# Two column blocks of an output projection by Strassen's seven products

## The chip, the core and the metric

One core of a Trainium2 chip. The metric is the device time of one execution in microseconds; lower is better. The runs of the kernel before took 1024.64, 1024.73 and 1025.47 us, median 1024.73.

## The reference

One layer of a hybrid encoder on 512 frames (tokens) of width 2048. One input projection feeds two groups of heads, RWKV-7 time mixing and an HGRN2 gated recurrence; their gated outputs are put side by side and go through one output projection, a scaled residual and a LayerNorm:

```python
proj = jnp.einsum('btd,dc->btc', h, w_in[l])
rw = _token_shift(proj[..., :RWKV_COLS], shift_mu[l])
hg = proj[..., RWKV_COLS:]
o_rwkv, v_first = _rwkv7_branch(rw, ...)
o_hgrn = _hgrn2_branch(hg, ...)
y = jnp.einsum('btc,cd->btd', jnp.concatenate([o_rwkv, o_hgrn], axis=-1), w_out[l])
h = _layer_norm(ALPHA * h + y, ln_w[l], ln_b[l])
```

The change lies in the last `einsum`: (512 x 2048) times (2048 x 2048), in float32.

## The kernel before, in words

**One wide matmul.** Float32 products are made of TensorE matmuls on `float32r` halves: every operand is split into a high part (a copy by ACT into `float32r`) and a low part (the rest, a subtraction by DVE), in `split` (L367 for ACT, L377 for DVE). `three` (L499) then issues high x high, high x low and low x high into the same PSUM bank. So a product of a 128x128 stationary tile and a 128x512 moving tile is three wide matmuls.

**Stages.** The head (L1317) multiplies the first pieces of x and of the weights while they arrive. Then come the input projections, one after another, each 48 wide matmuls by `proj` (L499); between them the planner places the narrow matmuls of the two recurrences (L353). Last comes the output projection, in four column blocks of 512 (d = 0 to 3). For d = 0, 1 and 2 all four token tiles are accumulated in four PSUM banks, and the loop goes over 16 depth steps: a weight tile of 128x512 serves 4 token tiles x 3 = 12 matmuls. The last block goes token tile by token tile, with its 16 weight tiles kept split in SBUF; they were loaded and split alternately with those of d = 2 (`_last_quarters`). Its last token tile is cut in two column halves for the last four depth steps, so that the serial chain behind the last matmul (statistics, LayerNorm, store) is short.

**What sets the order.** The Python program is a planner: class `Plan` keeps a clock for each engine, and generators in queues (`splits`, `evacs`, `sums`, ...) yield operations with an assumed cost. `three` advances PE's clock and calls `pump`, which issues whatever is ready by the clocks. The order on each engine is therefore fixed when the kernel is built. A narrow matmul is issued when its operands are due 0.35 us ahead (`LEAD`). At run time engines meet by semaphores alone, each in its own fixed order.

**Weights.** `load(j)` sends 512 KB (two weight tiles) from `w_all` into one of two `wr` buffers, on SP's queue, once the buffer two loads back has been split. The split tiles go into a ring of three `wh`/`wl` buffers. SP's queue also carries the head's pieces, all other loads, the spills (`spill`: 12 of the 16 gated outputs rest in DRAM until the output projection), the passes through DRAM that transpose (`far`), the residual (`x_r`) and the stores of the result.

**Evacuation.** `row_out` adds the scaled residual to the PSUM bank on DVE (L390) and writes a `y` tile; statistics follow (L1581), and `finish` normalizes a token tile once its last column block is in (DVE L377, ACT L1510). `finish_last` does so for the last tile.

GpSimd does little before: clears (L419), powers for the square roots (L416), and one addition of 128x512 in the tail (L409).

Of the kernel before, what the change touches and what calls it, by code (L numbers as in the profile page):

```python
# [7 lines left out]
F32 = mybir.dt.float32  # L8
# [7 lines left out]
P = 128  # L16
# [246 lines left out]
def mixer_kernel(ctx, tc, head, x_r, w_all, par, up, ln_wb, consts, hmask, out):  # L263
# [212 lines left out]
    def ready(i, home=None):

        if i < 2 * nload and i not in parts:
# [444 lines left out]
    def rwkv_scan(SS, sc):  # L923
# [16 lines left out]
        for c in range(NCH):  # L940
# [321 lines left out]

    us = [unit() for _ in range(FIRST)]
# [58 lines left out]
    for k in range(KT):  # L1322
# [60 lines left out]
    def split_gated(n):  # L1383
        while len(whole) < min(n, KT):
# [68 lines left out]
    lnw = []  # L1453
# [60 lines left out]
    def finish_last(t, pbs, weigh):  # L1514
# [4 lines left out]
        dg = st("ksq", [P, T])[:, :P]  # L1519
        yield from spread(t, mv, rs, 5)  # L1520
# [48 lines left out]

    def row_out(t, d, ps):  # L1570
        y = ys[t][d] = yt[4 * t + d]
        xr = xrs[t]
        k = y_keys(t, d * T, d * T + T)

        def run():
            yield keyed(stt(y, xr, ALPHA, ps, ALU.mult, ALU.add), [xr.tensor.name, ps.tensor.name], k + [y.tensor.name])
            drop(ps, xr)
            plan.add(sums, rest())

        def rest():  # L1580
            yield keyed(Op([("dve", 0.07 + T * 0.00105, lambda: dve.bn_stats(stats[:, t, d], y))], [], []),  # L1581
                        k, [f"stat{t}"])
            if d == 3:
                yield from finish(t)
            else:
                yield from premultiply(t, d)

        plan.add(evacs, run())

    xrs = {}  # L1590

    def residual(t, d):
# [11 lines left out]

    def ahead(j, d):

        if d == 0:
            split_gated(j + 2)
            if j == 8:
                plan.until(room(big=1))  # L1610
                lnw.append(take("big", [P, 2, D]))
                send(lnw[0], ln_wb[None].to_broadcast([P, 2, D]))
                plan.fetched(lnw[0], 8 * D)
# [4 lines left out]
    for d in range(2):  # L1618
        rows(4 * unit(4), T, gh, gl, lambda t, ps, d=d: fin(t, ps, d), korder, lambda j, d=d: ahead(j, d),
             banks if d else banks[:1])  # L1620

    q0 = 4 * unit(8)
    seq = _last_quarters()
    homes = {}

    def home(n):
        if n < 9:
            return lambda: tuple(take("t", (P, QT), F32R) for _ in range(2))  # L1630
        if n == 9:
# [5 lines left out]
        if n == 10:  # L1637
            return lambda: tuple(take("ksq", (P, QT), F32R) for _ in range(2))
        if n < 13:
            def both():  # L1640
                if not homes:
# [167 lines left out]
```

## Time and profile before

| | |
|---|---|
| median of three runs | 1024.73 us |
| the profiled execution | 1025.05 us |
| its span, first to last instruction | 1023.3 us |
| instructions | 18559 |
| granted TensorE clock, mean | 0.999 |
| HBM read, written | 111.08 MB, 18.48 MB |

The profile is one execution. Its engines are PE (TensorE matmuls), PEld (TensorE weight loads, which run beside PE), DVE (VectorE), ACT (ScalarE), POOL (GpSimd) and SP (SyncE, which issues DMAs). A group row has line, engine, operation, out<-in by tile names, shapes and count, then the busy time in us and the mean of one in ns, then the idle time before and who ended it. A timeline row has start and length in us. Matmuls overlap, so the length of one (393 ns) is not the distance to the next. "PEclk" is the granted clock as a share of full speed.

### The profile page before, as it was taken

How to read it: one execution, taken by the hardware profiler on the slowest of the kernel's cores; microseconds unless marked ns; L12 is line 12 of the kernel's file. 1: busy time of each engine (PE TensorE's matmuls, PEld its weight loads, DVE VectorE, ACT ScalarE, POOL GpSimd, SP SyncE). 2: the span in 40 equal slices, each digit the busy share in tenths (PEclk: the TensorE clock that was granted, in tenths of full speed). 3: DMA queues.
4: the chain of work that ended last, by engine and by line, in shares of the span. 5: the costliest groups of instructions: out<-in, count | busy, mean ns of one | idle time of the engine just before them, and what ended most of it. 6: DMA issues, size and time to landing. Idle time of an engine off the chain costs nothing.

```text
span 1023.3 us, 18559 instructions
## 1 busy us (share of the span) xinstructions
PE 1015.0 (99%) x7124; PEld 839.5 (82%) x7124; DVE 805.0 (79%) x1753; ACT 474.6 (46%) x879; POOL 42.8 (4%) x78
## 2 busy tenths in 40 slices
PE   9999999999999999999999999999999999999997
PEld 8888888888888878888888888888888878888885
DVE  7477999779779979888999867867999988526556
ACT  6456345546373454555534353636345554223321
POOL 0000001001000010010001000100001001000001
PEclk9999999999999999999999999999999999999999
DMA  9134452342535422335463333363343247445613
GB/s 340 54 103 129 124 143 83 96 124 88 177 106 155 124 84 63 100 113 166 121 182 105 100 98 116 106 187 103 119 128 94 78 142 237 144 119 169 202 55 134
DMA packets 58553, 130.77 MB, mean 128 GB/s; under 512 B 9824, under 2 KB 25440, under 8 KB 58336
## 3 DMA queue, kind: packets, MB, share of 16 engines
q1 hardware_dynamic: 58032, 128.67, 42.1%
q8 instruction: 56, 0.92, 0.4%
q10 hardware_dynamic: 432, 0.92, 0.3%
q14 instruction: 33, 0.27, 0.1%
HBM read 111.08 MB, written 18.48 MB: 127 GB/s over the span
## 4 chain that ended last, share of the span: by engine, by line
PE 95%; DVE 3%; issue 1%; DMA 0%; ACT 0%; DVEq 0%; ACTq 0%; SPq 0%
PE main L499 73%; PE mix L353 9%; PE mix L499 8%; PE main L1317 3%; PE main L353 2%; DVE t L377 1%; DVE wl L377 1%; PE mix L1268 0%; DMA t<-spill 0%; DVE bd L390 0%; DVE big L403 0%; DVE inv L403 0%; DVE zz L377 0%; PE mix L358 0%; DVE nr L398 0%
## 5 line engine op out<-in xcount | busy, mean ns | idle before, releaser
L499 PE MATMUL main<-xh,wh 128*128 128x512 f32 x864 | 339.8, 393 | 0.0
L499 PE MATMUL main<-xh,wl 128*128 128x512 f32 x864 | 339.5, 393 | 0.0
L499 PE MATMUL main<-xl,wh 128*128 128x512 f32 x864 | 338.9, 392 | 0.0
L367 ACT ACTIVATE wh<-wr 128x512 fp32r<-128x512 f32 x299 | 186.6, 626 | 190.0 <-PE main L499 128.6
L377 DVE TENSOR_TENSOR wl<-wr,wh 128x512 fp32r<-128x512 f32 x299 | 203.7, 683 | 61.6 <-ACT wh L367 57.4
L499 PEld LDWEIGHTS main<-xh,wl 128*128 128x128 f32 x864 | 162.3, 188 | 33.6
L499 PEld LDWEIGHTS main<-xh,wh 128*128 128x128 f32 x864 | 162.3, 188 | 32.9
L499 PEld LDWEIGHTS main<-xl,wh 128*128 128x128 f32 x864 | 162.4, 188 | 32.9
L499 PE MATMUL main<-wh,xh 128*128 128x512 f32 (+1 forms) x249 | 97.3, 391 | 0.0
L499 PE MATMUL main<-wl,xh 128*128 128x512 f32 (+1 forms) x249 | 97.0, 389 | 0.0
L499 PE MATMUL main<-wh,xl 128*128 128x512 f32 (+1 forms) x249 | 96.5, 388 | 0.0
L499 PEld LDWEIGHTS main<-wh,xh 128*128 128x128 f32 x249 | 46.8, 188 | 9.6
L499 PEld LDWEIGHTS main<-wh,xl 128*128 128x128 f32 x249 | 46.8, 188 | 9.4
L499 PEld LDWEIGHTS main<-wl,xh 128*128 128x128 f32 x249 | 46.8, 188 | 9.2
L368 ACT ACTIVATE t<-main,om 128x512 f32<-128x512 f32 x33 | 22.3, 685 | 46.0 <-PE main L499 35.5
L390 DVE SCALAR_TENSOR_TENSOR bd<-mix,pc,bd 64x64 f32<-64x64 f32 x112 | 31.7, 283 | 12.5 <-PE mix L353 10.4
L377 DVE TENSOR_TENSOR inv<-inv,inv 64x30 f32<-64x30 f32 (+14 forms) x120 | 38.5, 321 | 3.1
L377 DVE TENSOR_TENSOR inv<-inv 64x30 f32<-64x30 f32 (+14 forms) x120 | 38.4, 320 | 2.4
L390 DVE SCALAR_TENSOR_TENSOR t<-main,pr,t 128x511 f32<-128x511 f32 x33 | 24.3, 743 | 17.7 <-ACT t L368 17.3
L377 DVE TENSOR_TENSOR t<-t,tot 128x256 f32<-128x256 f32 x96 | 37.3, 417 | 0.3
L368 ACT ACTIVATE t<-main 128x512 f32<-128x512 f32 x32 | 18.6, 596 | 34.4 <-PE main L499 34.3
L367 ACT ACTIVATE t<-mix 64x128 f32<-64x128 f32 (+3 forms) x57 | 15.0, 267 | 41.1 <-DVE zz L377 25.5
(244 smaller groups left out, 1437.2 us busy)
## 6 DMA issues: line engine op xcount, KB each, us to landing
wr<-w_all SPq DMA_DIRECT2D x156, 512.0 KB, 3.6
q<-head SPq DMA_DIRECT2D x14, 448.0 KB, 5.6
far<-ksq SPq DMA_DIRECT2D x22, 256.0 KB, 3.7
far<-q SPq DMA_DIRECT2D x8, 512.0 KB, 3.7
q<-far SPq DMA_DIRECT2D x32, 128.0 KB, 4.6
g<-x_r SPq DMA_DIRECT2D x16, 256.0 KB, 4.1
t<-far SPq DMA_DIRECT2D x56, 64.0 KB, 3.5
spill<-g SPq DMA_DIRECT2D x12, 256.0 KB, 4.0
```

What stands on the lines that cost most here:

```text
L353: return Op([("pe", cost, lambda: pe.matmul(o, l, r, start=start, stop=stop, **kw))], [l, r], [o], mode=("narrow", l.shape[0], 32 if m <= ...
L367: return "act", cost, lambda: sc_e.activation(o, i, f, scale=scale)
L368: return "act", cost, lambda: sc_e.activation(o, i, f, scale=scale, bias=bias)
L377: return dve_op([a, b], o, lambda: dve.tensor_tensor(o, a, b, f), base=base or 0.16 if o.shape[0] < P and size(o) == C and o.tensor.name i ...
L390: return dve_op([a, b], o, lambda: dve.scalar_tensor_tensor(o, a, s, b, f1, f2), per=0.00113, base=0.085 if o.shape[0] == P and size(o) > ...
L499: pe.matmul(ps, l, r, start=first and i == 0, stop=last and i == 2)
L1317: pe.matmul(pss[a], *ops, start=k == 0 and low == of == 0, stop=k == KT - 1 and low == 1)
```

## The change

**Seven products.** Columns 512 to 1535 (d = 1 and 2) are one 512 x 2048 by 2048 x 1024 product. Depth is cut in two halves: depth tile 2m belongs to the first and 2m + 1 to the second, for m = 0 to 7. Tokens are cut into 0 to 255 and 256 to 511, columns into d = 1 and d = 2. Strassen's method (in Winograd's form) needs seven products of half-size matrices in place of eight. They are the seven passes in `PASSES`. Each goes over 8 depth steps and has 2 PSUM banks, one for each of 2 token tiles, so a weight tile serves 6 matmuls. Three passes use plain weights (`B11`, `B21`, `B22`) and four use sums of weights (0 to 3); three use plain tokens (`A11`, `A12`, `A22`) and four use sums of tokens (`S1` to `S4`). `gather` adds each pass's two banks to the `y` tiles on DVE.

**Weight sums.** `weight_sums`, two loops that start in the head, do this 16 times in all: load 512 KB of `w_all` into an `inv` buffer, form the sums by four subtractions of 128x256 on GpSimd, store 512 KB to `sums_w` in DRAM. All on SP's queue. The passes load the sums from there.

**Token sums.** `union` forms S1 to S4 by four GpSimd operations of 128x256 for each m, as soon as `split_gated` has split the two gated outputs; 12 of those are read a second time from `spill`. `alone` splits the sums into high and low.

**Buffers.** In the passes the ring of weights has a fourth buffer (in `ksq`) and the loads a third (in two `t` tiles, `third`).

**Residual and norm weights.** The residual of these two blocks is scaled by ACT and added to `y` by GpSimd (`join`, 8 additions of 128x512). The LayerNorm's weights are read in four parts after the token sums have been split (`fetch_norm`), no longer in one read in the first block; the early multiplications of the last token tile go into a queue of their own (`weighs`).

**Last block.** Token tiles 0 and 1 are accumulated together, 6 matmuls for a weight tile; tiles 2 and 3 follow as before.

**Elsewhere.** In the recurrence both PSUM banks of a step are taken before its two matmuls are issued.

```diff
+PASSES = (("B11", "A11"), ("B21", "A12"), (3, "S2"), (0, "S1"), ("B22", "S4"), (1, "S3"), (2, "A22"))
...
+            if j < joint or (j - joint) % 3 < 2:
+                t = st("wr", [P, HALF])
+                raws[j] = [t[:, :QT], t[:, QT:]]
+                send(t, source(j))
+                plan.fetched(t, 4 * HALF)
+            else:
+                raws[j] = third
+                for i, t in enumerate(third):
+                    send(t, source(j)[:, i * QT : i * QT + QT])
+                    plan.fetched(t, 4 * QT)
...
-                    load(i // 2 + 2)
+                    load(i // 2 + (2 if i // 2 < joint else 3))
...
+    def weight_sums(first):
+        yield room(inv=1)
+        w = take("inv", [P, 4, QT // 2])
+        for i in range(first, NSUM, 2):
+            m, h = divmod(i, 2)
+            yield lambda: plan.clock["sp"] <= plan.clock["pe"] + 0.2
+            send(w, w_all[nsent + i].rearrange("p (a c) -> p a c", a=4))
+            plan.fetched(w, 4 * HALF)
+            for o, a, b in ((0, 1, 0), (1, 3, 1), (3, 3, 0), (2, 2, 3)):
+                yield pool_tt(w[:, o], w[:, a], w[:, b], ALU.subtract)
+            yield lambda: by_now(w)
+            yield lambda: plan.clock["sp"] <= plan.clock["pe"] + 0.2
+            send(sums_w[:, :, m, h * QT // 2 : (h + 1) * QT // 2].rearrange("a p c -> p a c"), w)
+            there = plan.busy[w.tensor.name] = (plan.clock["sp"] + 4.5, "dma")
+            yield lambda: there[0] <= plan.clock["pe"]
+        drop(w)
...
+        yield pool_tt(d2[:, hi_t], r1[:, hi_t], r2[:, hi_t], ALU.add)
+        yield pool_tt(d1[:, hi_t], r1[:, lo_t], r1[:, hi_t], ALU.subtract)
+        yield pool_tt(d1[:, lo_t], d2[:, hi_t], r1[:, lo_t], ALU.subtract)
+        yield pool_tt(d2[:, lo_t], r2[:, lo_t], d1[:, lo_t], ALU.subtract)
...
+        yield act(xr, xr, AF.Copy, scale=ALPHA)
+        yield keyed(pool_tt(y, ya, xr, ALU.add), ka + [xr.tensor.name], k)
...
+    for p, (_, name) in enumerate(PASSES):
+        pss = []
+        for m in range(NPAIRS):
+            n = parts0 + p * NPAIRS + m
+            hi, lo = part(n, T)
+            for i in range(2):
+                if m == 0:
+                    pss.append(main_ps(banks))
+                prepared(n + 1 + 2 * i)
+                if i == 0:
+                    prepared(n + 2)
+                three(pss[i], *factor(name, m, i), hi[:, 0], lo[:, 0], m == 0, m == NPAIRS - 1)
...
+    for n in range(KT):
+        for t in range(2):
+            if n == 0:
+                pss.append(main_ps(banks))
+            three(pss[t], *shares(t, n, KT - 1))
+    for t in range(2):
+        row_out(t, 3, pss[t])
+    for t in (2, 3):
```

SP's queue behind the head, in the kernel before. `wr` are weights, `up` a small weight of the recurrence, and the brackets name the engines and DMA semaphores an issue waits for:

```order
L332 DMA wr_349<-w_all 128x1024 [waits DMAHW5_49]
L332 DMA wr_414<-w_all 128x1024 [waits DMAHW6_49,DMAHW3_49,DVE_49]
L332 DMA up_445<-up 128x256 [waits DMAHW7_49]
L332 DMA wr_489<-w_all 128x1024 [waits DMAHW5_49,DMAHW0_49,DVE_49]
L332 DMA up_532<-up 128x256 [waits DMAHW1_49,DMAHW7_49,DVE_49,Activation_49]
L332 DMA wr_561<-w_all 128x1024 [waits DMAHW6_49,DMAHW2_49,DVE_49]
```

The same place in the changed kernel; `inv_270` and `inv_271` are the buffers of the two loops:

```order
L332 DMA wr_355<-w_all 128x1024 [waits DMAHW7_49]
L332 DMA sums_w<-inv_270 128x4x256 [waits DMAHW0_49,Pool_49]
L332 DMA sums_w<-inv_271 128x4x256 [waits DMAHW1_49,Pool_49]
L332 DMA inv_270<-w_all 128x1024 [waits DMAHW2_49,DMAHW0_49]
L332 DMA wr_430<-w_all 128x1024 [waits DMAHW5_49,DMAHW3_49,DVE_49]
L332 DMA inv_271<-w_all 128x1024 [waits DMAHW4_49,DMAHW1_49]
L332 DMA up_464<-up 128x256
L332 DMA sums_w<-inv_270 128x4x256 [waits DMAHW6_49,DMAHW2_49,Pool_49]
L332 DMA wr_514<-w_all 128x1024 [waits DMAHW7_49,DVE_49]
L332 DMA sums_w<-inv_271 128x4x256 [waits DMAHW4_49,Pool_49]
L332 DMA inv_270<-w_all 128x1024 [waits DMAHW6_49]
```

A weight load now stands behind a store that waits for GpSimd and behind a reload that waits for that store.

PE in the block d = 2 of the kernel before, the end of one weight tile (`wh_9736`, `wl_9737`) and the start of the next; `xh`/`xl` are the gated outputs' halves, `main` and `mix` are PSUM banks:

```order
L499 MATMUL main_9707<-wh_9736,xh_8971 128x512
L499 MATMUL main_9707<-wl_9737,xh_8971 128x512
L499 MATMUL main_9707<-wh_9736,xl_8972 128x512
L499 MATMUL mix_9718<-wh_9736,xh_8971 128x512
L499 MATMUL mix_9718<-wl_9737,xh_8971 128x512
L499 MATMUL mix_9718<-wh_9736,xl_8972 128x512
L499 MATMUL main_9697<-wh_9759,xh_8998 128x512
```

PE in the second pass of the changed kernel, one whole weight tile and the start of the next, which lies in the fourth buffer (`ksq`):

```order
L524 MATMUL mix_9682<-wh_9736,xh_9418 128x512
L524 MATMUL mix_9682<-wl_9737,xh_9418 128x512
L524 MATMUL mix_9682<-wh_9736,xl_9419 128x512
L524 MATMUL mix_9689<-wh_9736,xh_9418 128x512
L524 MATMUL mix_9689<-wl_9737,xh_9418 128x512
L524 MATMUL mix_9689<-wh_9736,xl_9419 128x512
L524 MATMUL mix_9682<-ksq_9557,xh_9472 128x512
L524 MATMUL mix_9682<-ksq_9558,xh_9472 128x512
```

A weight tile serves two banks in place of four, so PE asks for the next one twice as soon.

DVE in the block d = 1 before, where it only splits weights (`wl`):

```order
L377 TENSOR_TENSOR inv_9384<-inv_9384,big_9206 128x512
L377 TENSOR_TENSOR wl_9437<-wr_9346,wh_9436 128x512
L377 TENSOR_TENSOR wl_9455<-wr_9397,wh_9454 128x512
L377 TENSOR_TENSOR wl_9471<-wr_9397,wh_9470 128x512
L377 TENSOR_TENSOR wl_9489<-wr_9443,wh_9488 128x512
```

DVE at the start of the first pass now; `big` holds token sums, the `t` tiles written with 256 columns are their low halves, `q` and `inv` are `y` tiles of the first block:

```order
L377 TENSOR_TENSOR wl_9592<-t_9507,wh_9591 128x512
L377 TENSOR_TENSOR t_9551<-big_9049,t_9551 128x256
L390 SCALAR_TENSOR_TENSOR inv_9519<-g_9542,mix_8991 128x512
L377 TENSOR_TENSOR wl_9617<-wr_9535,wh_9616 128x512
L377 TENSOR_TENSOR t_9607<-big_9049,t_9607 128x256
L377 TENSOR_TENSOR t_9552<-big_9049,t_9552 128x256
L377 TENSOR_TENSOR ksq_9558<-wr_9535,ksq_9557 128x512
```

Splits of the token sums and the first block's evacuations now stand between the splits of weights.

More of the change, by code (lines that the diff above doesn't have):

```diff
@@ new lines, in fetch_norm, with union_done @@
+    def fetch_norm():
+        yield room(big=1)
+        w = take("big", [P, 2, D])
+        for d in range(4):
+            c = slice(d * T, d * T + T)
+            send(w[:, :, c], ln_wb[None, :, c].to_broadcast([P, 2, T]))
+            plan.fetched(w, 8 * T)
+            now = plan.clock["pe"]
+            yield lambda: plan.clock["pe"] > now + 4.0
+        lnw.append(w)
+    def union_done(n):
+        now = plan.clock["pe"]
+        for m in range(NPAIRS):
+            t = homes[n, m]
+            if n in ("S1", "S3") and m < 4:
+                if m:
+                    continue
+                t = homes[n]
+            plan.busy[t.tensor.name] = (now, "pe")
+            drop(t)
+        homes[n, "free"] = True
@@ L1603, in fin, with extra @@
         row_out(t, d, ps)
+    def extra():
+        yield room(t=2)
+        third.extend([take("t"), take("t")])
+        load(joint + 2)
     def ahead(j, d):
@@ L1608, in ahead @@
             split_gated(j + 2)
[L1609 to L1613, printed above, removed]
+            if j == KT - 1:
+                plan.add(plan.queue(), extra())
         if 0 <= j - KT // 2 - 3 < 4:
@@ L1617, in mixer_kernel, with plus @@
     banks = ("main", "mix")
[L1618 to L1629, printed above, removed]
+    rows(4 * unit(4), T, gh, gl, lambda t, ps: fin(t, ps, 0), korder, lambda j: ahead(j, 0), banks[:1])
+    joins = plan.queue()
+    def plus(o, a, ps):
+        y, k = ys[o[0]][o[1]], y_keys(o[0], o[1] * T, o[1] * T + T)
+        ya, ka = ys[a[0]][a[1]], y_keys(a[0], a[1] * T, a[1] * T + T)
+        return keyed(tt(y, ya, ps, ALU.add), ka + [ps.tensor.name], k)
@@ new lines, in mixer_kernel, with home, kept @@
+    for o in ((0, 1), (1, 1), (2, 2), (0, 2), (3, 2), (1, 2), (2, 1), (3, 1)):
+        residual(*o)
+    parts0 = 4 * unit(NPASS * NPAIRS // 4)
+    single0 = 4 * unit(4)
+    fourth = []
+    def home(i):
+        n = i - single0
+        if n < 0:
+            if (i - parts0) % 4 < 3:
+                return None
+            def kept():
+                if not fourth:
+                    fourth.extend(take("ksq", (P, QT), F32R) for _ in range(2))
+                for t in fourth:
+                    plan.busy[t.tensor.name] = (over.get(i - 4, 0.0), "pe")
+                return tuple(fourth)
+            return kept
+        if n < 8:
@@ L1636, in home @@
             return one
[L1637 to L1639 removed]
+        if n < 12:
             def both():
[L1641 to L1650 removed]
@@ L1652, in mixer_kernel @@
[L1652 to L1664 removed]
+                if "last" not in homes:
+                    homes["last"] = take("ia", (P, 4, QT), F32R)
```

267 lines of the change are left out of this document (202 added, 65 removed).

## The prediction

> **What bounds the kernel now.** I read the page's busy shares first, then the waits of PE, then busy time by stretches, then the timelines of DVE, ACT and GpSimd, and the DMA issues. The page's shares (busy us, share of the span, instructions):
>
> ```profile
> PE   1015.0 (99%) x7124; PEld 839.5 (82%) x7124; DVE 805.0 (79%) x1753; ACT 474.6 (46%) x879; POOL 42.8 (4%) x78
> ```
>
> PE is busy for all but 8.3 us of 1023.3. Its longest wait is one of 1.1 us in the whole program, and the last block ends in a serial chain behind the last wide matmul (waits of PE; then the end of the chain, start and length in us):
>
> ```profile
> PE mix L353 <- ACT ksq L1547: 1.1, 1, 1.1
> ```
> ```profile
> 1010.68 2.87 PE main L499 x24
> 1013.55 0.02 issue
> ...
> 1018.88 0.39 DVEq L1805
> ```
>
> So the time is the number of PE instructions times their pitch, plus a head and a tail that this change leaves alone. The pitch of a wide matmul comes from DVE's evacuations of the first token tile of two successive column blocks, which are 192 matmuls apart:
>
> ```profile
> 880.46 0.69 DVE L390 SCALAR_TENSOR_TENSOR q<-g,main 128x512 f32<-128x512 f32 x1 [2.04 <-PE main L499]
> ...
> 921.24 0.69 DVE L377 TENSOR_TENSOR wl<-wr,wh 128x512 fp32r<-128x512 f32 x1 [2.03 <-ACT wh L367]
> ...
> 923.98 0.69 DVE L390 SCALAR_TENSOR_TENSOR q<-g,main 128x512 f32<-128x512 f32 x1 [2.04 <-PE main L499]
> ```
>
> (923.98 - 880.46) / 192 = 0.2267 us. Twelve matmuls on one weight tile are 2.72 us, and inside a block DVE sits idle about 2.03 us of each: the old output projection leaves DVE and ACT most of their time. The stretches say the same (columns: PE, PEld, DVE, ACT, POOL busy, granted clock, DMA share, GB/s):
>
> ```profile
> core 0: us, PE busy (x) PEld busy (x) DVE busy (x) ACT busy (x) POOL busy (x), PEclk, DMA share, GB/s
> 20.00:126.00 106.00, 106.00 (x513) 87.50 (x512) 77.03 (x139) 57.28 (x95) 0.27 (x2) 1.00 0.38 116
> ...
> 879.50:923.00 43.50, 43.50 (x194) 36.02 (x193) 16.46 (x25) 10.12 (x16) 0.00 (x0) 1.00 0.41 121
> ```
>
> DVE is busy 16.46 of 43.50 us there, the granted clock is 1.00.
>
> **The matmuls taken away.** Columns 512 to 1535 cost 2 x 192 = 384 wide matmuls. Seven products of 8 half-depth steps, 2 token tiles and 3 partial products are 336. 48 x 0.2267 = **10.9 us less**, all on the path. The stationary loads stay hidden: one takes 188 ns, under the 227 of its matmul.
>
> ```profile
> L499 PEld LDWEIGHTS main<-xh,wl 128*128 128x128 f32 x864 | 162.3, 188 | 33.6
> ```
>
> Everything else in the change is cover that must hold. I go through it in program order.
>
> **The weight sums, early.** GpSimd makes 64 subtractions of 128x256. The nearest rows are its one wide subtraction-like instruction and two small ones, with what DVE ran beside them:
>
> ```profile
> 855.25 1.01 POOL L416 TENSOR_TENSOR rs<-rs,mhalf 128x4 f32<-128x4 f32 x1 [6.72 <-DVE rs L387]
> 858.49 1.51 POOL L416 TENSOR_TENSOR rs<-rs,mhalf 128x4 f32<-128x4 f32 x1 [2.23 <-DVE rs L387]
> ...
> 1017.01 1.78 POOL L409 TENSOR_TENSOR inv<-inv,big 128x512 f32<-128x512 f32 x1 [1.42 <-ACT inv L1551]
> ```
> ```profile
> 858.45 0.69 DVE L377 TENSOR_TENSOR wl<-wr,wh 128x512 fp32r<-128x512 f32 x1
> ...
> 1016.92 0.75 DVE L390 SCALAR_TENSOR_TENSOR inv<-inv,rs,big 128x512 f32<-128x512 f32 x1
> 1017.59 1.68 DVE L390 SCALAR_TENSOR_TENSOR inv<-inv,rs,mix 128x512 f32<-128x512 f32 x3
> ```
>
> Half of 1.78 is 0.89 us, 57 us in all; if the 0.58 us until DVE's next instruction (1017.59) were a wait, half of 1.20 is 0.60, or 38 us. I take 0.89. [...]
>
> What the sums can hurt is SP. Two loops take turns: load 512 KB, subtract four times, store 512 KB, load again. Each store waits on GpSimd, and each reload on its store, in the one SP queue that also carries the weights. In the order, 15 weight loads lie between the first and the last store of one loop (`inv_270`), which is 7 rounds; a load feeds 24 wide matmuls. How long those take early on, narrow matmuls included, comes from the counts of the stretch 20 to 126:
>
> ```profile
> L499 PE MATMUL main<-xh,wh 128*128 128x512 f32 x118 | 46.1, 391 | 0.0
> L499 PE MATMUL main<-xh,wl 128*128 128x512 f32 x118 | 46.0, 390 | 0.0
> L499 PE MATMUL main<-xl,wh 128*128 128x512 f32 x118 | 46.0, 389 | 0.0
> L1317 PE MATMUL main<-xh,t 128*128 128x512 f32 x57 | 14.5, 389 | 0.0
> L1317 PE MATMUL main<-xl,t 128*128 128x512 f32 x27 | 7.6, 389 | 0.0
> ```
>
> 438 in 106 us is 0.242 each; 15 x 24 x 0.242 / 7 = **12.4 us that the order allows for a round**. What a round needs (size and median us to landing on the page, then the landing spread of `wr` between 20 and 140 and one row of the DMA issues between 20 and 126):
>
> ```profile
> wr<-w_all SPq DMA_DIRECT2D x156, 512.0 KB, 3.6
> ...
> far<-q SPq DMA_DIRECT2D x8, 512.0 KB, 3.7
> ```
> ```profile
> DMA to landing us min/median/max: 3.4/3.6/4.6
> ```
> ```profile
> q<-far SPq DMA_DIRECT2D x4, 128.0 KB, 4.7
> ```
>
> At best 3.6 + 4 x 0.89 + 3.7 = 10.9 us. At worst 4.6 + 4 x (0.89 + 0.60) + 4.7 = 15.3, each subtraction behind one DVE instruction and the store of 1 KB pieces as slow as `q<-far`. I take 12.7, nearer to the first, because the same 512 KB shapes are quoted at 3.6 and 3.7. DMA adds 16 x 1.05 = 16.8 MB over 106 us, 158 GB/s on top of 116, 274 in all; the head runs at 340:
>
> ```profile
> GB/s 340 54 103 129 124 143 83 96 124 88 177 106 155 124 84 63 100 113 166 121 182 105 100 98 116 106 187 103 119 128 94 78 142 237 144 119 169 202 55 134
> ```
>
> A late SP queue does not reach PE at once. Splits run ahead by a ring of three weight tiles (ACT, then DVE):
>
> ```profile
> 64.34 0.63 ACT L367 ACTIVATE wh<-wr 128x512 fp32r<-128x512 f32 x1 [0.24 <-PE main L499]
> 67.06 0.63 ACT L367 ACTIVATE wh<-wr 128x512 fp32r<-128x512 f32 x1 [2.09 <-PE main L499]
> ```
> ```profile
> 65.83 0.68 DVE L377 TENSOR_TENSOR wl<-wr,wh 128x512 fp32r<-128x512 f32 x1
> ```
>
> A split begins when PE leaves a buffer, ends 2.2 us later (64.34 to 66.51), and PE wants it after two tiles, 5.4 us: 3.2 spare. The reload issued at 2.2 lands at 5.8 and is wanted at three tiles, 8.2: 2.4 spare. Together 5.6 us. Eight rounds at 12.7 are late by 8 x 0.3 = 2.4, inside that: nothing. At 10.9 also nothing; at 15.3, 8 x 2.9 - 5.6 = 17.6 us. What isn't covered by this lead are narrow matmuls, which the planner places 0.35 us behind their operands (`LEAD`). A DVE chain late by one subtraction (0.89) costs about 0.5 there, and the stretch has three such places (the key-norm sums, the decay products, the score products): **1.5 us**, with 0 and 17.6 as ends. The first loads of the sums also go ahead of the last four pieces of x and weights at the start; 1 MB at 340 GB/s is 3.1 us there, and with 34 us of head matmuls for 21 us of its transfers (7.3 MB) it is covered: nothing. The loops hold both `inv` buffers, so the first pair's solve starts later in the order; from the 960th wide matmul on the narrow ones stand in both orders in the same numbers again: nothing.
>
> **Unions, in the first block.** 32 GpSimd instructions of 128x256 and 12 more reads of 256 KB run beside 43.5 us in which DVE has 27 us free. Nothing, except for the eight that are queued as late as the first pass.
>
> **The seven passes.** They last 336 x 0.2267 = 76.2 us, and a weight tile now serves 6 matmuls, 1.36 us. DVE's start-to-start times are 0.60 us for 512 columns and 0.33 for 256:
>
> ```profile
> 253.07 0.67 DVE L377 TENSOR_TENSOR t<-t,sm 128x512 f32<-128x512 f32 x1
> 253.67 0.15 DVE L387 TENSOR_SCALAR sm<-sm 128x8 f32<-128x8 f32 x1
> ```
> ```profile
> 841.45 0.42 DVE L377 TENSOR_TENSOR t<-t,tot 128x256 f32<-128x256 f32 x1
> 841.78 0.69 DVE L377 TENSOR_TENSOR xl<-t,xh 128x512 fp32r<-128x512 f32 x1
> ```
>
> The order has 119 DVE instructions in the passes, 32 of them the 256-column splits: 87 x 0.60 + 32 x 0.33 = 62.8 us, 82%. The fullest passes are the first, 15 x 0.60 + 5 x 0.33 = 10.7 of 10.9 us, and the fifth, 13 and 8, 10.4. Four weight tiles of lead less a split are 4 x 1.36 - 2.2 = 3.2 us. If no GpSimd instruction holds DVE up, nothing is lost. If each does, 8 union steps (7.1) and 8 residual sums (8 x 1.78 = 14.2) make 84.1 against 76.2 + 3.2: 4.7 us. I take **1.2**, nearer to nothing, because the row at 858.49 has GpSimd as the one that waits (1.51 against 1.01, under DVE's instruction of 858.45) and because the unions are wanted only two passes later. DMA: 28 loads, 8 residuals and the norm weights are 18.9 MB in 76.2 us, 248 GB/s, again under 340.
>
> **The last block.** Same matmuls. Token tiles 0 and 1 end together, which puts 16 norm instructions of 0.60 (9.6 us) beside tile 2's 48 matmuls (10.9): covered, and the tail of 1013.55 to 1023.3 stays. The later fetch of the norm weights has two blocks' worth of time.
>
> **Sum.** The profiled execution took 1025.05: 1025.05 - 10.9 + 1.5 + 1.2 = 1016.85. The median of the runs shown lies 0.32 below the profiled one: **1016.5**.
>
> **The rivals.**
> - *All covered*, neither loss: 1025.05 - 10.9 - 0.32 = 1013.8. For it: PE waits of 1.1 us at most in a program planned the same way. Against it: GpSimd work beside DVE is new. 0.13.
> - *GpSimd and DVE shut each other out.* Every GpSimd instruction with SBUF inputs delays the next two-input DVE instruction by its whole length: 4.7 us in the passes, and in the early stretch 57 us of GpSimd next to 77.0 of DVE in 106, 28 too many, of which a tenth to a fifth (3 to 5 us) reaches PE through the narrow matmuls. 1013.8 + 4.7 + 3 = 1021.5. For it: 858.49. Against it: no row shows DVE waiting. 0.18. [...]
> - *SP falls behind the sums* (slower than before). A round of 15.3 us delays the weights by 17.6: 1013.8 + 17.6 = 1031.4. It decides from 12.4 + (10.9 + 5.6) / 8 = 14.5 us a round. For it: SP takes everything in order and the allowance has 1.5 us in it. Against it: the quoted landings. 0.11.
> - *The matmuls are not saved*: 1024.7. The order counts 3828 wide ones against 3876. 0.02.
>
> **How the numbers follow.** The forecast has the remaining 0.56. Low end: all covered less 0.4 for the spread of the terms, 1013.4. High end 1022.0, past the second rival's 1021.5; left out are the third (0.11), the fourth (0.02) and a tail of the second (0.04). A measurement of this kernel can tell about 0.2%, 2.0 us, from no change. Faster by more: 0.56 + 0.13 + 0.14 = 0.83. Within: 0.07 (0.03 of the second, 0.02 each of the third and fourth). Slower: 0.10.
>
> **What would show it.** Right: PE busy near 1004, early waits of PE under 2 us, SP's stores of `sums_w` never waiting long on GpSimd, the seven passes in 76 to 78 us. Wrong: wide matmuls in 20 to 150 us waiting on DVE `wl` behind a late `wr` (third rival), DVE instructions of 128x512 that last over 1 us beside GpSimd (second), or a pass longer than 12 us.

## The result, and the profile after

The changed kernel takes **1039.1 us** (median of 4 runs, 1038.53 to 1040.78) against 1024.8 for the kernel before on the same chip: ratio 1.0141, interval 1.0124 to 1.0159. It is slower by 14.3 us. The forecast was 1016.5 with a range of 1013.4 to 1022.0. The profiled execution took 1039.38 us.

The page of the changed kernel, busy shares:

```profile
PE 1012.2 (98%) x7076; PEld 830.2 (80%) x7076; DVE 859.5 (83%) x1815; ACT 499.8 (48%) x945; POOL 151.3 (15%) x182
```

PE has 48 instructions less, as it should, yet stays busy for 1012.2 us of a span of 1037.4. The waits of PE (in total, times, longest) say where it stood:

```profile
PE main L524 <- DVE wl L377: 5.8, 4, 2.1
PE mix L353 <- DVE ksq L377: 4.2, 3, 2.2
PE main L353 <- DVE q L377: 2.9, 2, 1.6
PE mix L353 <- ACT ksq L1680: 2.7, 1, 2.7
```

Before, no wait was longer than 1.1 us. Now PE waits for DVE in the first three rows, in front of wide matmuls (weight splits `wl`) and of narrow ones (L353), and the tail has 2.7 where it had 1.1. The stretches of the changed kernel, columns as in the prediction; the second is that of the seven passes:

```profile
20.00:126.00 106.00, 98.82 (x475) 80.23 (x475) 81.12 (x110) 54.10 (x89) 54.45 (x61) 1.00 0.77 247
891.10:981.40 90.30, 83.20 (x338) 64.16 (x337) 73.43 (x119) 48.35 (x100) 29.67 (x27) 0.96 0.73 238
```

In 20 to 126 PE was busy 106.00 us before and does 38 instructions less now, while DVE is busy 81.12 us for 110 instructions (before 77.03 for 139), so they take longer on average. The passes last 90.3 us where 76.2 were reckoned; one by one, counted by 48 wide matmuls each: 14.6, 11.5, 13.2, 11.1, 15.1, 11.5, 13.3. Four of the seven are over the 12 us that the prediction named as a sign of being wrong.

**A table of losses.** For each PE instruction I took the distance to the start of the next one, less the median distance for its shape in the trace before, and summed this by stretch (us). Total before 37.3, now 62.2: 24.9 more. With 10.9 saved that is 14.0; the spans differ by 14.1. So nothing is missing from the account; it says where time was lost and not yet why. The rows below the second are the experiments. The first column is the median time. The losses are those of the one profiled execution, which lies up to 1.9 us off the median, and 3.1 in e6_sums_dve; the 2.5 to 3.2 us lost ahead of 20 us are not listed.

| kernel | time | 20-126 | 126-860 | 860-980 | from 980 |
|---|---|---|---|---|---|
| before | 1024.8 | 0.9 | 30.4 | 0.0 | 3.0 |
| changed | 1039.1 | 9.3 | 30.5 | 14.7 | 5.1 |
| e1_no_sub | 1033.1 | 0.9 | 34.3 | 13.6 | 4.8 |
| e2_clears | 1033.8 | 0.9 | 31.6 | 14.7 | 6.1 |
| e3_joins_dve | 1032.6 | 9.6 | 32.3 | 7.2 | 4.9 |
| e4_joins_unions_dve | 1032.9 | 8.3 | 30.9 | 8.4 | 5.7 |
| e5_all_dve | 1040.1 | 1.4 | 41.1 | 10.8 | 7.4 |
| e6_sums_dve | 1044.9 | 1.6 | 39.5 | 16.1 | 4.7 |
| e7_all_dve_res | 1035.9 | 1.4 | 41.3 | 7.2 | 7.3 |
| e8_pool_sums_res | 1035.2 | 9.1 | 31.2 | 9.1 | 7.2 |
| e9_no_sub_res | 1028.0 | 0.9 | 32.3 | 10.5 | 4.7 |
| e10_three_subs | 1034.5 | 0.9 | 34.8 | 13.4 | 6.2 |
| e11_twelve_four | 1033.3 | 1.6 | 38.1 | 10.1 | 6.0 |
| e12_no_rereads | 1022.8 | 0.9 | 30.5 | 5.3 | 4.8 |
| e13_no_rereads_no_first | 1023.5 | 0.9 | 33.2 | 5.9 | 6.0 |
| e14_no_sub_joins | 1027.0 | 0.9 | 32.7 | 7.4 | 6.0 |

The kernel before was between 1025.0 and 1025.3 (medians) beside the experiments.

**Early.** DVE, GpSimd and PE of the changed kernel, around the longest early wait:

```profile
85.00 2.26 DVE L406 TENSOR_TENSOR ksq<-t 32x512 f32<-32x512 f32 x2
87.29 1.12 DVE L377 TENSOR_TENSOR wl<-wr,wh 128x512 fp32r<-128x512 f32 x1
88.33 1.22 DVE L377 TENSOR_TENSOR pf<-pf,ksq 64x512 f32<-64x512 f32 x1
90.30 1.18 DVE L377 TENSOR_TENSOR ksq<-pf,ksq 64x512 fp32r<-64x512 f32 x1 [0.76 <-ACT ksq L367]
```
```profile
85.64 1.07 POOL L409 TENSOR_TENSOR inv<-inv 128x256 f32<-128x256 f32 x1
...
88.04 4.03 POOL L409 TENSOR_TENSOR inv<-inv 128x256 f32<-128x256 f32 x4 [0.18 <-DMA inv<-w_all]
```
```profile
91.62 0.47 PE L353 MATMUL mix<-ksq,ones_r 128*128 128x512 f32 x1 [2.20 <-DVE ksq L377]
```

DVE's two-input instructions of 512 columns last 1.12 to 1.22 us in place of 0.68, the subtractions 1.0 in place of the 0.74 to 0.76 that one of that size takes while DVE stands (889.01 to 891.08). The chain that ends in `ksq` is late by several such delays of 0.44 to 0.54 us, and PE stands 2.20 us.

**In the passes.** The same three engines when four residual additions come close together:

```profile
942.74 1.21 DVE L377 TENSOR_TENSOR ia<-big,ia 128x256 fp32r<-128x256 f32 x1
943.87 1.78 DVE L377 TENSOR_TENSOR ksq<-t,ksq 128x512 fp32r<-128x512 f32 x1
945.57 1.52 DVE L377 TENSOR_TENSOR ia<-big,ia 128x256 fp32r<-128x256 f32 x1
947.01 1.50 DVE L377 TENSOR_TENSOR t<-zz,t 128x256 fp32r<-128x256 f32 x1
948.43 0.41 DVE L377 TENSOR_TENSOR ia<-big,ia 128x256 fp32r<-128x256 f32 x1
948.77 0.68 DVE L377 TENSOR_TENSOR wl<-wr,wh 128x512 fp32r<-128x512 f32 x1
```
```profile
942.37 2.73 POOL L409 TENSOR_TENSOR q<-q,g 128x512 f32<-128x512 f32 x2 [18.26 <-DVE q L377]
945.06 1.74 POOL L409 TENSOR_TENSOR inv<-q,g 128x512 f32<-128x512 f32 x1
946.88 1.34 POOL L409 TENSOR_TENSOR q<-q,g 128x512 f32<-128x512 f32 x1
```
```profile
949.50 0.50 PE L524 MATMUL main<-wl,t 128*128 128x512 f32 x1 [2.14 <-DVE wl L377]
```

Four DVE instructions take 6.0 us in place of 1.95 (0.42, 0.69, 0.42, 0.42). The weight split behind them begins 4.1 us late, more than the lead of 3.2, and PE stands 2.14 us.

**At the start of the passes** it is not DVE that is busy. GpSimd, SP and DVE rows:

```profile
879.44 4.06 POOL L409 TENSOR_TENSOR big<-t,t 128x256 f32<-128x256 f32 x1 [1.82 <-DMA t<-spill]
```
```profile
889.08 2.42 SPq L332 DMA_DIRECT2D g<-x_r  x2
```
```profile
886.54 1.21 DVE L377 TENSOR_TENSOR wl<-wr,wh 128x512 fp32r<-128x512 f32 x1 [0.64 <-ACT wh L367]
892.17 0.69 DVE L390 SCALAR_TENSOR_TENSOR q<-g,main 128x512 f32<-128x512 f32 x1 [4.42 <-DMA g<-x_r]
892.89 0.70 DVE L1705 BATCH_NORM_STATS2 stats<-q 128x6 f32<-128x512 f32 x1
893.50 1.07 DVE L377 TENSOR_TENSOR wl<-wr,wh 128x512 fp32r<-128x512 f32 x1
```

A token sum lasted 4.06 us under back-to-back DVE instructions, the later ones held the `g` buffers until 889.05, the residual was read late, DVE stood 4.42 us in front of the evacuation, and the weight split queued behind it came late for PE (2.15 us from start to start at 892.47). A short stretch behind that wait shows one thing more, the granted clock:

```profile
894.00:899.00 5.00, 4.38 (x12) 3.36 (x13) 4.06 (x6) 1.89 (x5) 3.70 (x5) 0.66 1.00 368
```

From 895.7 to 898.7 matmuls stood 0.427 us apart in place of 0.227, and so again from 950.4 to 953.4. Each time that is 7 or 8 matmuls by 0.2, 1.5 us on top of the wait.

### The profile page after: what moved, and what is told of

It reads as the page before. It is cut to its first block, busy times and chain, and to the rows that moved or that the text cites. A ratio compares the mean times of both kernels' runs of the same rounds, so it can differ in the third digit from the quotient of the medians.

```text
span 1037.4 us, 18856 instructions
## 1 busy us (share of the span) xinstructions
PE 1012.2 (98%) x7076; PEld 830.2 (80%) x7076; DVE 859.5 (83%) x1815; ACT 499.8 (48%) x945; POOL 151.3 (15%) x182
## 4 chain that ended last, share of the span: by engine, by line
PE 80%; DVE 10%; DMA 4%; issue 3%; ACT 1%; POOL 1%; SPq 0%; DVEq 0%; ACTq 0%; POOLq 0%
PE main L524 64%; PE mix L353 9%; PE main L1359 3%; DVE wl L377 2%; DVE q L377 2%; PE mix L524 2%; PE main L353 2%; DMA t<-spill 1%; DMA wr<-sums_w 1%; DVE t L377 1%; DMA g<-x_r 1%; DMA q<-far 1%; DMA q<-head 1%; DVE g L390 1%; DVE ksq L377 0%
## 5 line engine op out<-in xcount | busy, mean ns | idle before, releaser
L367 ACT ACTIVATE wh<-wr 128x512 fp32r<-128x512 f32 x293 | 182.6, 626 | 177.5 <-PE main L524 131.5
L524 PE MATMUL main<-wl,xh 128*128 128x512 f32 x200 | 78.9, 395 | 2.7 <-DVE wl L377 2.7
L524 PE MATMUL main<-wh,xh 128*128 128x512 f32 x200 | 78.9, 395 | 0.0
L524 PE MATMUL main<-wh,xl 128*128 128x512 f32 x200 | 78.5, 392 | 0.3 <-DVE xl L377 0.3
L409 POOL TENSOR_TENSOR inv<-inv 128x256 f32<-128x256 f32 x64 | 59.8, 937 | 73.3 <-DMA inv<-w_all 69.8
L416 POOL TENSOR_TENSOR sm<-sm,mhalf 128x8 f32<-128x8 f32 x8 | 18.5, 2318 | 200.8 <-DVE sm L386 150.7
L524 PEld LDWEIGHTS main<-wl,xh 128*128 128x128 f32 x200 | 37.7, 188 | 11.4 <-DVE wl L377 3.8
L524 PEld LDWEIGHTS main<-wh,xl 128*128 128x128 f32 x200 | 37.7, 189 | 8.3 <-DVE xl L377 0.7
L524 PEld LDWEIGHTS main<-wh,xh 128*128 128x128 f32 x200 | 37.7, 188 | 7.9
L390 DVE SCALAR_TENSOR_TENSOR bd<-mix,pc,bd 64x64 f32<-64x64 f32 x112 | 31.7, 283 | 10.5 <-PE mix L353 8.3
```

The source lines that it names most:

```text
L367: return "act", cost, lambda: sc_e.activation(o, i, f, scale=scale)
L390: return dve_op([a, b], o, lambda: dve.scalar_tensor_tensor(o, a, s, b, f1, f2), per=0.00113, base=0.085 if o.shape[0] == P and size(o) > ...
L409: return "pool", 0.1 + size(o) * 0.0029, lambda: pool.tensor_tensor(o, a, b, f)
L416: lambda: pool.tensor_tensor(o, i, mhalf[:, : size(o)], ALU.pow))], [i], [o])
L524: pe.matmul(ps, l, r, start=first and i == 0, stop=last and i == 2)
```

## The experiments

Theories: **1**, GpSimd instructions that read SBUF and DVE instructions with two SBUF inputs exclude each other. **2**, SP's queue and the transfers make weights and operands late. **4**, DVE has simply too much to do. **5** came up later: the order that the planner makes. (3, the granted clock, fell behind waits of PE, as above, and was not tried by itself.)

### e1_no_sub and e2_clears: what costs early

```diff
-yield pool_tt(w[:, o], w[:, a], w[:, b], ALU.subtract)
+yield Op([("pool", 0.1 + 256 * 0.0029, lambda: None)], [w], [w])     # e1_no_sub
...
+def clears(o=o):                                                      # e2_clears
+    for _ in range(3):
+        pool.memset(w[:, o], 1.0)
...
+yield Op([("pool", 0.1 + 256 * 0.0029, clears)], [w], [w])
```

> The 64 weight-sum subtractions on GpSimd are left out, so the products of four passes use unsummed weights; every load and store of the sums stays, and so does the order. In the changed kernel PE loses 8.1 us between 40 and 120 us (wide matmuls behind DVE). Theory 1 (GpSimd and DVE shut each other out): with no GpSimd work there DVE's 128x512 two-input instructions go back to 0.68 us, the early loss falls to 0.5 to 1 us and the time from 1039.1 to about 1031.5. Theory 2 (the SP queue and the transfers: stores, reloads and weights share one queue and the DMA engines): the transfers are all still there, 4 us or more of the early loss stay, and the time is over 1035. The late loss is the same by both.

> Each weight-sum subtraction is replaced by three clears of the same 128x256 piece on GpSimd, which write SBUF and read nothing; the products of four passes so use wrong weights. SP's stores still wait for GpSimd and GpSimd is about as busy. Theory 1 (it is the reading of SBUF by GpSimd that excludes DVE's two-input instructions): early loss 0.5 to 1.5 us, about 1031.5 to 1032.5, DVE's 128x512 back at 0.68 us. Theory 2 (stores of SP waiting on GpSimd delay weights): the early loss stays at 6 us or more, about 1037 to 1040.

Measured: 1033.1 (ratio to before 1.008, 1.0065 to 1.0095) and 1033.8 (1.0091, 1.0069 to 1.0113). The early loss falls from 9.3 to 0.9 in both, to what it was before. The largest group of DVE between 40 and 120, before, in the changed kernel, in e1_no_sub, then in e2_clears with its GpSimd row between 15 and 130 (busy us, mean ns of one):

```profile
L377 DVE TENSOR_TENSOR wl<-wr,wh 128x512 fp32r<-128x512 f32 x26 | 17.8, 684 | 5.9 <-ACT wh L367 3.9 <-PE main L499 1.8
```
```profile
L377 DVE TENSOR_TENSOR wl<-wr,wh 128x512 fp32r<-128x512 f32 x23 | 19.0, 828 | 6.8 <-ACT wh L367 6.6
```
```profile
L377 DVE TENSOR_TENSOR wl<-wr,wh 128x512 fp32r<-128x512 f32 x27 | 18.5, 684 | 10.7 <-ACT wh L367 8.5 <-PE main L524 1.8
```
```profile
L377 DVE TENSOR_TENSOR wl<-wr,wh 128x512 fp32r<-128x512 f32 x27 | 18.4, 683 | 10.0 <-ACT wh L367 8.0 <-PE main L524 1.8
```
```profile
L1299 POOL MEMSET inv<- 128x256 f32 x191 | 57.3, 316 | 70.2 <-DMA inv<-w_all 62.9
```

SP's own waits between 15 and 130, in the changed kernel and in e2_clears:

```profile
SPq L332 <- POOL inv L409: 23.1, 12, 4.2
```
```profile
SPq L332 <- POOL inv L1299: 29.1, 12, 5.3
```

e2_clears decides: GpSimd is busy 57.3 us there, SP's stores wait for it longer than in the changed kernel, all transfers run, and DVE's 828 ns go back to 683. So theory 1 holds for the early loss and theory 2 falls there. Both times are 1 to 2 us above the expectation: a gap of 2.8 and 1.7 us from start to start appears at 133, so the kernels gain 6.1 and 5.3 us and not the whole 8.4.

### e3_joins_dve and e4_joins_unions_dve: what costs late

```diff
-yield act(xr, xr, AF.Copy, scale=ALPHA)
-yield keyed(pool_tt(y, ya, xr, ALU.add), ka + [xr.tensor.name], k)
+yield keyed(stt(y, xr, ALPHA, ya, ALU.mult, ALU.add), ka + [xr.tensor.name], k)
...
-yield pool_tt(d2[:, hi_t], r1[:, hi_t], r2[:, hi_t], ALU.add)        # e4 alone, and the three after it
+yield tt(d2[:, hi_t], r1[:, hi_t], r2[:, hi_t], ALU.add)
```

> The 8 residual sums of the passes are made by one DVE instruction each (scale and add), not by ACT and then GpSimd; nothing is left out. DVE gets 8 x 0.60 = 4.8 us more work of its own. Theory 1 (exclusion): each GpSimd addition of 128x512 now costs DVE up to 1.1 us, so DVE is freer than before by 4 us; the stalls of 1.34, 2.54, 1.29 and 1.31 us between 920 and 976 and one of two drops of the granted clock (1.7 us) go: about 1031 to 1034. Theory 4 (DVE is simply too full with 1.36 us for a weight tile): the passes get longer by 1 to 4 us, 1040 to 1043.

> The 8 residual sums and the 32 steps of the token sums (128x256) are all on DVE; GpSimd keeps the weight sums alone. Nothing is left out. Theory 1 (exclusion): nothing holds DVE or GpSimd off late any more; the stall of 2.15 us at 892 with the clock drop behind it goes too, the late loss falls from 14.9 to under 4 us, about 1026 to 1029, and the early loss of 8 us stays. Theory 4 (DVE too full): 32 x 0.33 + 8 x 0.60 = 15.4 us more on DVE makes the block and the passes longer, 1039 to 1045.

Measured: 1032.6 (1.0068, 1.0051 to 1.0084) and 1032.9 (1.0075, 1.006 to 1.009). e3_joins_dve is as theory 1 has it: DVE got more to do and PE lost 7.5 us less (14.7 to 7.2). The passes of e3_joins_dve:

```profile
893.80:974.90 81.10, 78.98 (x338) 62.40 (x337) 69.74 (x124) 45.54 (x92) 16.16 (x17) 1.00 0.82 263
```

81.1 us in place of 90.3, DVE busy 69.74 for 124 instructions in place of 73.43 for 119, the clock at 1.00. The run also takes 8 scalings off ACT and changes the late order, which no run separates; but DVE's own splits got shorter, as theory 1 has it: `ksq<-wr,ksq` (ten of 128x512) falls from 868 to 735 ns on average, `ia<-big,ia` (eight of 128x256) from 650 to 414. Theory 4 falls as the explanation of this part. e4_joins_unions_dve missed: no gain over e3_joins_dve where 4 us or more were expected. The token sums on GpSimd were not what the rest hung on: DVE still stands 3.0 us there for the residual (`g<-x_r`) and 2.1 for second reads (`t<-spill`), so the long token sum was not the only reason why the residual came late.

### e5_all_dve, e6_sums_dve, e7_all_dve_res: the weight sums on DVE

```diff
-yield pool_tt(w[:, o], w[:, a], w[:, b], ALU.subtract)
+yield tt(w[:, o], w[:, a], w[:, b], ALU.subtract)                    # e5 (on e4), e6 (alone), e7 (on e4)
...
+yield keyed(copy(y, ps), [ps.tensor.name], k + [y.tensor.name])      # e7: first block, in row_out's place
+drop(ps)
+plan.add(joins, join((t, d)))
```

> Weight sums, token sums and residual sums all on DVE; GpSimd does what it did in the kernel before. Nothing is left out. The kernel with only the token and residual sums on DVE took 1032.9 us and still lost 7 us early. Theory 1 (exclusion): DVE takes 64 x 0.33 = 21 us for the weight sums itself, where the exclusion cost it about 0.55 us on each of its own 128x512 instructions; the early loss falls from 7 to 0.5 to 3 us, about 1026 to 1029. Theory 4 (DVE too full, early too: 77 of 106 us before): the narrow matmuls wait as long for DVE's own work as for the exclusion, 1031 to 1035.

> Only the 64 weight-sum subtractions are moved to DVE; token sums and residual sums stay on GpSimd. Nothing is left out. Theory 1 (exclusion): early loss 0.5 to 3 us in place of 8.1, the late loss stays near 12 to 15 us, 1032 to 1034.5, near the kernel without the subtractions (1033.05). Theory 4: 1036 to 1040.

> As the one with all sums on DVE, and the first column block leaves PSUM by a plain copy; its residual is added afterwards on DVE, as in the passes, so that DVE no longer waits 3 to 4.4 us for the residual's transfer in front of weight splits at 892. Nothing is left out. Theory 2 in its late form (loads issued late in SP's queue are what remains once the exclusion is gone): the stalls of about 1.9, 0.9 and 2.2 us between 890 and 906 shrink to under 2 in all, 2 to 4 us under the kernel with all sums on DVE, about 1023 to 1026. If DVE's fullness sets the remaining late loss, no change or slower.

Measured: 1040.1 (1.0148, 1.0133 to 1.0163), 1044.9 (1.0185, 1.017 to 1.02) and 1035.9 (1.0109, 1.0092 to 1.0126). All three times missed; only the difference of e7_all_dve_res to e5_all_dve, 4.2 us, is near the 2 to 4 expected, with the late loss 3.6 us smaller. The early loss did go, to 1.4 to 1.6, with DVE busy 81.5 of the 106 us, so DVE was not too full there. But 126 to 860 now loses 39.5 to 41.3 us in place of 30.5, though the last weight sum ends by 173. Most of that lies at one place, the same in all three: a wait of 4.99 us, with the clock at half for 6.8 us from about its end on (PE of e7_all_dve_res, then the stretch around it):

```profile
484.74 2.52 PE L353 MATMUL main<-q,q 64*128 64x128 f32 x15 [4.99 <-DVE t L390]
```
```profile
478.00:495.00 17.00, 12.01 (x63) 9.94 (x62) 16.94 (x34) 4.40 (x9) 4.50 (x4) 0.80 0.47 138
```

That stretch loses 7.8 to 8.6 us in the three and 0.1 in the changed kernel. DVE has hardly a pause in it (16.94 of 17.00 us, 14.53 in the changed kernel), and the weight sums ended 300 us earlier: PE waits for DVE work of the recurrence that the order puts together there. The DVE instructions of the sums change what the planner places where, and hence the whole order behind; this one is worse. That is theory 5.

### e8_pool_sums_res to e11_twelve_four: adding up

All four have token and residual sums on DVE and the first block's plain copy. They differ in the weight sums: on GpSimd, left out, three DVE instructions a round, or twelve rounds on DVE and four on GpSimd.

```diff
+yield tt(w[:, 0:2], w[:, 1:4:2], w[:, 0:2], ALU.subtract)                     # e10, for the first two
+yield (tt if i < 12 else pool_tt)(w[:, o], w[:, a], w[:, b], ALU.subtract)    # e11
```

> Weight sums on GpSimd as in the changed kernel; token sums and residual sums on DVE, and the first block leaves PSUM by a plain copy with its residual added later. Nothing is left out. Up to 860 us its order is that of the changed kernel. Theory 1 with theory 2 late (exclusion early, late transfers in front of evacuations): the kernel with token and residual sums on DVE took 1032.9, and 4.6 us of its loss lay between 860 and 905; the plain copy takes 3 to 4.5 us of that: 1028.5 to 1030. If the copy brought nothing: 1033.

> As the one before, with the 64 weight-sum subtractions left out (four passes use unsummed weights); loads, stores and order stay. It is what the change would bring if the sums cost nothing on any engine. If the parts add up (early exclusion 7 to 8 us, late exclusion and late residual 9 to 11 of the 14 us lost): 1020 to 1023, 2 to 5 us under the kernel before. If something else than these parts makes up the loss: 1025 or more.

> All sums on DVE with the late residual, as the one of 1035.9, but the first two weight-sum subtractions of a round are one DVE instruction of 128x512 (3 in place of 4 in a round). Nothing is left out. Theory 5 (with the sums on DVE the loss between 126 and 860, 41 us against 30 before, comes from the order that the planner makes from 160 on, and not from DVE's share): a slightly different set of instructions gives another order, and the loss there falls by 3 to 7 us, 1029 to 1033. Theory 4 (DVE's share): 16 x 0.06 us less work on DVE is nothing, 1035 to 1037.

> As the first of this group, with the weight sums of the first twelve rounds (48 subtractions) on DVE and of the last four (16) on GpSimd. Nothing is left out. Theory 1: a quarter of the early loss of 8 us stays, 2 to 3 us, and theory 5: the order after 160 is near that of the changed kernel, plus 1 us: 1023 to 1027. Theory 4 (48 subtractions make DVE too full early): 1031 to 1036.

Measured: 1035.2 (1.0101, 1.0085 to 1.0116), 1028.0 (1.0039, 1.0022 to 1.0056), 1034.5 (1.01, 1.0085 to 1.0115) and 1033.3 (1.0081, 1.0066 to 1.0096). The plain copy brought nothing (e8_pool_sums_res is 2.3 over e4_joins_unions_dve). e9_no_sub_res missed: weight sums that cost nothing would still leave the kernel 3 us slower than before, with 10.5 us lost between 860 and 980. e10_three_subs lost 6.5 us less in 126 to 860 than e7_all_dve_res (34.8 against 41.3), as theory 5 has it: the wait of 4.99 us is gone, and 478 to 495 loses 0.5. It gave most of that back late, so its time lies between the two ranges, in neither. e11_twelve_four missed by theories 1 and 5: it loses 7.6 us more in 126 to 860 than the changed kernel. Its time is in theory 4's range, but not for theory 4's reason, as the early loss is 1.6. Most of the loss, 6.6 us, lies between 126 and 200, where GpSimd makes its four rounds (137.9 to 161.9). DVE's splits beside them last up to 1.21 us again, and PE then waits for DVE, with the clock at half for 3.4 us from about the end of that wait on:

```profile
162.39 0.87 PE L353 MATMUL mix<-q,t 128*32 128x48 f32 x32 [3.19 <-DVE q L377]
```

So that part fits the exclusion, moved to a place where it costs more, rather than the order.

What DVE stood for in e9_no_sub_res between 860 and 985:

```profile
DVE wl L377 <- ACT wh L367: 5.6, 5, 1.9
DVE big L377 <- DMA t<-spill: 4.2, 2, 2.5
...
DVE q L390 <- DMA g<-x_r: 2.8, 1, 2.8
DVE zz L377 <- DMA t<-spill: 2.6, 2, 1.3
```

9.6 us in front of reads: second reads of spilled outputs (6.8) and a residual (2.8), with weight splits behind them in DVE's order.

### e12_no_rereads, e13_no_rereads_no_first, e14_no_sub_joins: late reads

```diff
+r1, r2 = (gh[korder[2 * m + i]].bitcast(F32) for i in range(2))   # e12, e13: no send(r, spill[...])
...
-plan.add(joins, join((t, d)))                                     # e13: first block's residual
+plan.add(sums, rest(t, d))
...
-residual(j - KT // 2 - 3, d)
+pass
```

> As the kernel without the weight-sum subtractions and with the other sums on DVE (1028.0 us), and besides the 12 second reads of spilled gated outputs are left out: the token sums are formed from the high parts that lie in SBUF, so they lack the low parts. DVE and PE have the same instructions. That kernel still lost 10.5 us between 860 and 980 against the kernel before, while DVE stood 6.8 us in front of token sums and 2.8 in front of a residual sum, waiting for transfers, with weight splits queued behind. Theory 2 late (DVE's fixed order stands still for late reads): the late loss falls to 4 to 7 us, 1021.5 to 1025. Theory 4 (DVE's share of the passes): the same work is there, 1027 to 1029.

> As the one before, and the residual of the first column block is left out too (4 reads of 256 KB and 4 DVE sums less). Theory 2 late: no read is waited for in front of splits any more, the late loss falls to 1 to 4 us, 1018 to 1021.5, under the kernel before. Theory 4: 4 x 0.60 us less on DVE, at most 2 us under the one before.

> The changed kernel without the 64 weight-sum subtractions (left out, as in the first experiment) and with the 8 residual sums on DVE; the token sums stay on GpSimd and the first block takes its residual as before. The two gains measured singly were 6.1 and 6.5 us. If the early and the late exclusion are separate losses they add up: 1039.1 - 12.6 = 1026.5, 1025 to 1028. If they share a cause (the clock, the transfers): 1029 or more.

Measured: 1022.8 (0.9978, 0.9965 to 0.999), 1023.5 (0.9987, 0.9973 to 1.0) and 1027.0 (1.0015, 1.0002 to 1.0028). e12_no_rereads: the same work on DVE and PE and 12 reads less save 5.2 us, and the late loss halves (10.5 to 5.3). DVE's waits there have no DMA left:

```profile
DVE wl L377 <- ACT wh L367: 12.6, 9, 3.7
DVE zz L377 <- ACT zz L367: 3.2, 1, 3.2
DVE ia L377 <- ACT ia L367: 0.6, 1, 0.6
```

The weights did not land sooner for it: `wr<-sums_w` took 4.8 us from issue to landing in e9_no_sub_res (median, 860 to 985) and 5.9 here. So the second reads, with DVE's waits for them, are a cause by themselves. The run frees their `t` buffers too; that share is not separated. e13_no_rereads_no_first missed: the residual added nothing to it. e14_no_sub_joins is where the sum of the two single gains had it, 1026.5 expected and 1027.0 measured: early and late exclusion are separate losses.

No kernel that does the whole computation comes below the kernel before; the nearest is e3_joins_dve.

## Why the prediction was wrong

- **The matmuls taken away: right.** 3828 wide ones against 3876, and the account closes with the 10.9 us.
- **The weight sums, early: wrong in size.** The first step that failed is "A DVE chain late by one subtraction (0.89) costs about 0.5 there, and the stretch has three such places". The price of a subtraction was near (64 of them last 937 ns on average), but four come back to back for about 4 us, each two-input DVE instruction of 512 columns in that time lasts 1.12 to 1.22 us in place of 0.68, and a chain has several. PE waited five times, 1.4 us each (4.2 and 2.9 us in the rows of the result), and the stretch lost 8.4 us more in place of 1.5 (e1_no_sub, e2_clears).
- **The round of the loops: not what decided.** Sixteen stores from 25.1 to 135.8 us are 110.7 / 7.5 = 14.8 us a round, more than the 12.7 taken and the 14.5 of the third rival; with the early loss gone it is still 14.3 and 14.0 (e1_no_sub, e2_clears). No early wait of PE goes back to a late `wr`, and e2_clears, with SP's waits for GpSimd in place, loses nothing early. The rival's mechanism didn't come about.
- **The seven passes: wrong, and the largest miss.** The second step that failed is "I take 1.2, nearer to nothing, because the row at 858.49 has GpSimd as the one that waits." One row of one order was taken for a rule; in the passes DVE waits just as much (1.78, 1.52, 1.50 in the rows above). The upper end, 4.7, was wrong too: it set the delays of the whole 76 us against them and one lead of 3.2, as if they were spread evenly. Four additions within 6 us delay DVE by 4.1 at once. Measured: 7.5 us for the residual additions, the drops of the clock among it (e3_joins_dve), out of 14.7 us lost between 860 and 980.
- **The unions, put at "Nothing": wrong, though not by their own time.** The prediction weighed the 12 second reads against DVE's free time, but DVE has to wait for them, with weight splits queued behind. For the passes 248 GB/s were held against 340, and the time from issue to landing was not looked at: 5.4 us for `wr<-sums_w` on the page, where 3.6 stood for weights before. In e9_no_sub_res to e12_no_rereads the second reads are worth 5.2 us.
- **The last block: wrong by 2.1 us.** The prediction has it that "the tail of 1013.55 to 1023.3 stays". Now DVE still does the norm of tile 2 when the last bank is ready. The last wide matmul starts at 1013.25 before and at 1025.63 now, and DVE's second half of the last evacuation starts 0.32 us behind it before and 1.95 now; PE's wait for ACT in the tail (L1547, now L1680) is 1.1 us before and 2.7 now (DVE before, then in the changed kernel):

```profile
1006.11 5.01 DVE L377 TENSOR_TENSOR q<-q,big 128x512 f32<-128x512 f32 x8 [0.88 <-ACT q L1510]
1013.57 0.42 DVE L377 TENSOR_TENSOR inv<-inv,main 128x256 f32<-128x256 f32 x1
```
```profile
1020.92 3.81 DVE L377 TENSOR_TENSOR q<-q,big 128x512 f32<-128x512 f32 x6 [0.28 <-ACT q L1642]
1027.58 0.41 DVE L377 TENSOR_TENSOR inv<-inv,mix 128x256 f32<-128x256 f32 x1
```

This is read from the rows; no run was made for it.

- **The second rival** had the mechanism and 1021.5. DVE's 128x512 splits averaged 828 ns beside subtractions, 684 without them (e1_no_sub) and 683 beside clears, which write SBUF and read nothing (e2_clears). Its "by its whole length" is more than the early rows show: 0.44 to 0.54 us for each DVE instruction of 512 columns, where a subtraction by itself would take about the 0.74 to 0.76 of a token sum of that size. The rival was too cheap for the same two reasons, chains early and clusters late, and it had nothing for the second reads.

The sum of the prediction put 2.7 us of loss against the 10.9 saved; the table has 24.9. Of the 14.7 us between 860 and 980, 7.5 are shown for the residual additions and 5.2, in kernels without the rest, for the second reads. Some 5 us stay lost in e12_no_rereads. DVE stands for ACT's half of the splits there, and ACT for weights; ACT's longest waits between 860 and 985:

```profile
ACT wh L367 <- DMA wr<-sums_w: 16.0, 8, 3.8
ACT wh L367 <- PE mix L524: 9.6, 10, 1.6
ACT wh L367 <- DMA wr<-w_all: 5.4, 5, 2.5
```

That speaks for late weights as the rest, theory 2 once more, but no run took them away: it stays open. So does why the order of e5_all_dve to e7_all_dve_res costs 9 to 11 us more between 126 and 860; some 8 of them lie at the one place shown.

## What to carry to other kernels

GpSimd was not a free second DVE here: its subtractions of 128x256 made DVE's two-input instructions of 512 columns 0.44 to 0.54 us longer, and four additions of 128x512 put DVE back by 4.1 us. Count such instructions as time of DVE's too, and look where they cluster, since a lead covers one cluster and not an average. With an in-order engine that feeds the critical one, look at what stands ahead of the feeding instruction: a late read in front of a weight split made PE wait for a split that was not late by itself. And in a planned order each part of a change reshuffles the rest, so measure the parts by leaving them out, with the order kept.

## What the runs showed of the hardware

- Beside 57.3 us of clears on GpSimd DVE's 128x512 splits lasted 683 ns on average (e2_clears), as long as without them (684 in e1_no_sub); beside the subtractions of the changed kernel they averaged 828, and the one at 87.29 took 1.12 us. DVE instructions with one input in PSUM kept their length beside the subtractions (DVE and GpSimd of the changed kernel: these two last 0.67 us each, 0.68 on average without subtractions; the two-input one of 64x512 behind them, at 114.29, lasts 1.15):

```profile
112.99 1.27 DVE L377 TENSOR_TENSOR big<-mix,cst 128x512 f32<-128x512 f32 x2
```
```profile
112.52 3.50 POOL L409 TENSOR_TENSOR inv<-inv 128x256 f32<-128x256 f32 x4 [2.41 <-DMA inv<-w_all]
```

- It goes both ways: the token sum at 879.44 lasted 4.06 us while five DVE instructions followed each other at 0.60, where such a sum takes 0.74 to 0.76 while DVE stands.
- The granted clock fell to half behind some gaps of PE of 2.2 to 2.6 us from start to start (idle for 1.8 to 2.2 of it): in the changed kernel it is 0.50 for 3.41 us each, from 895.59 to 899.00 and from 950.20 to 953.61. Over all profiles there are 20 gaps of 2.0 to 2.8 us, ahead of the tail, with wide matmuls behind them, and these stood 0.427 us apart behind 8 of them; behind the 2.54 us at 946.96 they did, behind the 2.59 at 89.04 in the same run they did not, and behind the same gap of 2.59 at 89.02 in e3_joins_dve they did (clock 0.98 over 20 to 120 there, 1.00 over 20 to 126 in the changed kernel).
